# Descending columns in the projections' matmuls of a one-layer hybrid decoder trunk

## The chip, the cores and the metric

The kernel runs on one core of one Trainium2 chip. A core has five engines with instruction streams of their own: PE (TensorE, the 128 x 128 matmul array), DVE (VectorE), ACT (ScalarE), POOL (GpSimd) and SP (SyncE, which only issues transfers here). They work on SBUF, an on-chip memory of 128 partitions; PE writes its results to PSUM, eight banks of 512 fp32 columns in each partition. Off-chip memory is reached by DMA. The metric is the device time of one execution in microseconds (us), lower is better.

A matmul instruction has two operands. The stationary one (`lhsT`, 128 columns) is put into the array by a weight load, which the profile lists apart as PEld. The moving one (`rhs`, up to 512 columns) is then streamed past it column by column, and for every column that goes in, one column of results comes out and is written to, or added onto, a column of a PSUM bank. Where the moving columns are read and where the results go is told by two access patterns, each a start and a list of [step, count].

## The reference

One layer (`DEPTH` = 1), a batch of one, 256 tokens, width 1024, all in fp32. Three token mixers share one input projection; their outputs are gated and merged, and a squared-ReLU MLP with a gated per-layer embedding follows.

```python
proj = x @ w_in[i]                                   # 1024 -> 3528 columns
aq, ak, av, iq, ik, iw, bq, bk, bv, cq, ck, cv = jnp.split(proj, SPLIT_POINTS, axis=-1)
o_a = dsa_mixer(...)        # indexer, top-64 keys, 6 heads over one shared key/value head
o_b = dilated_mixer(...)    # 3 dilations x 4 slots
o_c = moba_mixer(...)       # one block of 256: plain causal attention, 6 heads
gates = jax.nn.sigmoid(x @ w_gate[i]).reshape(bsz, s_len, N_BRANCH, D_MODEL)
merged = (gates[:, :, 0] * (o_a @ w_br_a[i]) + gates[:, :, 1] * (o_b @ w_br_b[i])
          + gates[:, :, 2] * (o_c @ w_br_c[i]))
x = layer_norm(ALPHA * x + merged @ w_out[i], ln1_g[i], ln1_b[i])
h = jnp.square(jax.nn.relu(x @ w_up[i])) @ w_down[i]     # 1024 -> 4096 -> 1024
ple = jax.nn.sigmoid(x @ w_ple_gate[i]) * (p[i] @ w_ple[i])
x = layer_norm(ALPHA * x + h + ple, ln2_g[i], ln2_b[i])
```

By far the most arithmetic is in the products with weights: `w_in`, `w_gate`, `w_br_*`, `w_out`, `w_ple_gate`, `w_ple`, `w_up` and `w_down`. These are what the change calls the projections.

## The kernel before

Every fp32 product is computed from operands cut in two. `hi` is the value rounded to the array's reduced fp32 format (`F32R`), `lo` is what is left over, and a product a·b is the sum of three matmuls: hi·hi, hi·lo and lo·hi. Activations are cut once, when they are made. Weights are cut as they come in: the class `Weights` loads a unit of 128 x 1024 into one of five `raw` buffers (SP's DMA queue), ACT copies it with rounding to `whi` (L75), and DVE, in the first 58 units together with POOL, subtracts to get `wlo` (L79). `W.get` keeps four units ahead of the matmuls.

Nearly all matmuls come out of one helper, `prod` (L139 to L145), which emits the three matmuls of one 128 x 128 block: L141 hi·hi, L144 hi·lo and L145 lo·hi. Who calls it, in order of the program:

- `gemm`, for features and gates: stationary the weights, moving `xh`/`xl` (the transposed input, 256 tokens wide), results in one of three `mm` banks; `fill("c")` does the same with the mixers' outputs `op`.
- `values`, for the value heads: stationary the tokens, moving 328 or 384 weight columns.
- `merge` (256 columns), then the class `Wide` for `w_out` and the gate `w_ple_gate`, and the product with `w_ple`: stationary a tile of 128 tokens, moving 512 weight columns, results in banks that stay open over all eight blocks.
- The down projection (`onto`, `plain` and the last loop): stationary the hidden activations `hT`, moving 512 weight columns (a few 256). For 14 of the 32 hidden blocks, taken in pairs, it uses seven products in place of eight (Strassen-Winograd), with the sums made on DVE and POOL.

The up projection has its own two lines. At L825 `x1[:, :, k]` moves, 512 columns that are hi and lo of 256 tokens, so that one matmul does hi·hi and hi·lo into the two halves of a bank; at L827 the 256 hi columns move past the weights' `lo`. There the moving columns lie in two runs of 128 with a gap between them, and the results too.

Not through `prod` go the first four features (L429), the logits (L288), the transposes (L328, L676) and the product of probabilities and values (L332, L333).

The framework's scheduler sets the order of each engine's instructions when the kernel is built, and puts a semaphore wait ahead of an instruction wherever an operand was last touched elsewhere.

Of the kernel before, what the change touches and what calls it, by code (L numbers as in the profile page):

```python
# [98 lines left out]
def hybrid_layer(ctx: ExitStack, tc: tile.TileContext, x0, xn, pT, wqk, wva, wvb, wg, wbc, wba,  # L99
                 wout, wup, wdn, wpg, wple, lnrow, rel, onehot, pick, out):  # L100
    nc = tc.nc
    pe, act, dve, pool = nc.tensor, nc.scalar, nc.vector, nc.gpsimd
# [33 lines left out]

    pin = tc.keep_in_program_order

    def prod(ps, a, b, first, last, hold=False, more=False):  # L139

        i = pe.matmul(ps, lhsT=a[0], rhs=b[0], start=first, stop=False, skip_group_check=more)  # L141
        if hold:
            pin(i)
        pe.matmul(ps, lhsT=a[0], rhs=b[1], start=False, stop=False, skip_group_check=more)  # L144
        pe.matmul(ps, lhsT=a[1], rhs=b[0], start=False, stop=last, skip_group_check=more)  # L145

    def gemm(ps, units, xs, k=0):

        for u in units:
            hi, lo = W.get(u)  # L150
            for o in range(0, hi.shape[1], 128):
                prod(ps, (hi[:, o:o + 128], lo[:, o:o + 128]), xs[k], k == 0, k == len(xs) - 1)
                k += 1
# [57 lines left out]
    def mmbank(shape):  # L211
        t = mm.tile([128, 512], F32, name="mm", tag="mm")
        return t[:, 0:256] if shape == 256 else t
# [21 lines left out]
    def k_pair(a, b=None):  # L235


        k = (kp if b is None else k1).tile([128, 2, S], F32R, name="k", tag="k")
        for d, ps in ((slice(0, 128), a),) if b is None else ((slice(0, 64), a),
                                                             (slice(64, 128), b)):  # L240
            freed(act.copy(k[d, 0], ps),
                  dve.tensor_tensor(k[d, 1], ps, k[d, 0].bitcast(F32), op=ALU.subtract))
        return k
# [3 lines left out]
    def fill(what):  # L247


        for w in what:  # L250
            if w == "g":
                ps = mmbank(256)
                gemm(ps, u_g[n_g[0]], xs)
                freed(act.activation(G[:, n_g[0]], ps, AF.Tanh, scale=0.5))
                n_g[0] += 1
                continue
            f = n_c[0]
            n_c[0] += 1
            hi, lo = W.get(u_bc[f][0])
            ps = mmbank(512).rearrange("p (i s) -> p i s", i=2)  # L260
            for i, (k0, k1) in enumerate(((3, 5), (5, 8))):
                for k in range(k0, k1):
                    c = slice((k - 3) * 128, (k - 2) * 128)
                    prod(ps[:, i], (hi[:, c], lo[:, c]), (op[:, k, 0], op[:, k, 1]), k == k0,
                         k == k1 - 1)
            g = G[:, 3 * f + 1:3 * f + 3]
            freed(dve.scalar_tensor_tensor(g, g, 1.0, ps, op0=ALU.add, op1=ALU.mult))
            dve.tensor_tensor(g[:, 0], g[:, 0], g[:, 1], op=ALU.add)

    def feat(f):  # L270
        ps = mmbank(256)
        gemm(ps, u_q[f], xs)
        if f > 4:
            next(side, None)
        return ps
# [22 lines left out]
    def values(units, n, h0, heads, withiw):  # L298
        pss = [mmbank(512) for _ in range(2)]
        for i in range(4):  # L300
            hi, lo = W.get(units[i])
            for j in range(2):
                k = 2 * i + j
                c = slice(j * n, (j + 1) * n)
                for b in range(2):
                    t = slice(b * 128, (b + 1) * 128)
                    prod(pss[b][:, :n], (xh[:, k, t], xl[:, k, t]), (hi[:, c], lo[:, c]),
                         k == 0, k == KT - 1)
        v_out(pss, n, h0, heads, withiw)
# [98 lines left out]
    with ExitStack() as begin:  # L408
# [17 lines left out]
        for k in range(KT):  # L426
            for i, (w, x) in enumerate(((sh, xh), (sh, xl), (sl, xh))):
                for f in range(FIRST):
                    pe.matmul(first[f], lhsT=w[:, k, 128 * f:128 * f + 128], rhs=x[:, k],  # L429
                              start=k == i == 0, stop=k == KT - 1 and i == 2)  # L430
# [3 lines left out]
    ps = feat(4)  # L434
# [37 lines left out]
    for j in range(2):  # L472
        ps = feat(5 + 4 * j)
        k = k_pair(ps)
# [18 lines left out]
    for j in range(3):  # L493
        ps = feat(13 + 2 * j)
        k = k_pair(ps)
# [123 lines left out]
    x1 = p3.tile([128, 2, KT, 2, 128], F32R, name="x1", tag="x1")  # L619
# [68 lines left out]
    for i in range(4):  # L688
# [3 lines left out]
        b, cs = i // 2, H[i % 2]  # L692
        t = slice(b * 128, (b + 1) * 128)
        ps = mmbank(512)
# [79 lines left out]
    def load(i):  # L774

        wr[i] = r = xr[:, i % 2] if i else p3.tile([128, 2, D], F32, name="rows", tag="rows")
        k1, k2 = PAIRS[i]
        nc.sync.dma_start(r[:, 0], wdn[k1])
        for h in range(2):
            nc.sync.dma_start(r[:, 1, H[h]], wdn[k2, :, H[1 - h]])  # L780

    def form(i):

        t = p3.tile([128, 2, D], F32, name="rows", tag="rows") if i % 2 else Y
        wt[i] = t = t.rearrange("p b d -> p (b d)")
        r = wr[i].rearrange("p b d -> p (b d)")
        dve.tensor_tensor(t[:, 0:1024], r[:, 512:1536], r[:, 0:1024], op=ALU.subtract)
        dve.tensor_tensor(r[:, 512:1024], r[:, 1024:1536], t[:, 0:512], op=ALU.subtract)
        dve.tensor_tensor(t[:, 1024:1536], r[:, 1536:2048], r[:, 512:1024], op=ALU.subtract)
# [18 lines left out]
    def relu2(dst, ps):  # L808
        dve.tensor_reduce(dst, ps.rearrange("p b a t -> p b t a"), axis=AX.X, op=ALU.add)  # L809
        act.activation(dst, dst, AF.Relu)  # L810
        act.activation(dst, dst, AF.Square)  # L811
# [3 lines left out]
    for f in range(32):  # L815
        if f == 16:
            with tc.issue_after(W.loads[-1]):
                load(0)
            with tc.issue_after(W.subs[-1]):
                form(0)  # L820
        ps = mmbank(512).rearrange("p (b a t) -> p b a t", b=2, a=2)
        hi, lo = W.get(u_up[f][0])
        cs = [slice(k * 128, (k + 1) * 128) for k in range(KT)]
        for k, c in enumerate(cs):
            pe.matmul(ps, lhsT=hi[:, c], rhs=x1[:, :, k], start=k == 0, stop=False)  # L825
        for k, c in enumerate(cs):
            pe.matmul(ps[:, :, 0], lhsT=lo[:, c], rhs=x1[:, :, k, 0], start=False,  # L827
                      stop=k == KT - 1)
        if f not in half_of:
            spare = f % 2 == 0  # L830
            q = (p3.tile([128, 2, 128], F32, name="q1", tag="q1") if spare else
                 w2.tile([128, 8, 128], F32, name="a8", tag="a8")[:, 0:2])
            relu2(q, ps)
            q = q.rearrange("p b t -> p (b t)")
            act.copy(hT[f][:, 0], q)
            dve.tensor_tensor(hT[f][:, 1], q, hT[f][:, 0].bitcast(F32), op=ALU.subtract)
            continue
        j = half_of[f].index(f)
        if j == 0:
            a8 = w2.tile([128, 8, 128], F32, name="a8", tag="a8")  # L840
        relu2(a8[:, 2 * j:2 * j + 2], ps)
        if j == 0:
            continue

        a21, a11, a22, a12, *sums = (a8[:, j] for j in range(8))
        pool.tensor_tensor(sums[0], a21, a22, op=ALU.add)
        pool.tensor_tensor(sums[1], sums[0], a11, op=ALU.subtract)
        pool.tensor_tensor(sums[2], a11, a21, op=ALU.subtract)  # L848
        pool.tensor_tensor(sums[3], a12, sums[1], op=ALU.subtract)
        h = hT[half_of[f]]  # L850
        q = a8[:, 1:8].rearrange("p j t -> p (j t)")
        act.copy(h[:, 0], q)
        dve.tensor_tensor(h[:, 1], q, h[:, 0].bitcast(F32), op=ALU.subtract)
# [16 lines left out]
    def weights(u):  # L870
        w = W.get(u)
        while later:
            i = later.pop(0)
            load(i)
            form(i)
        return w
# [9 lines left out]
    for k in SEQ[:-2]:  # L886
# [3 lines left out]
        for u, terms in zip(u_dn[k], TERMS):  # L890
            hi, lo = weights(u)
# [27 lines left out]
    for i, acc in enumerate(ends):  # L919
        c = slice(256 * i, 256 * i + 256)  # L920
# [28 lines left out]
    for b in range(2):  # L949
        t = slice(128 * b, 128 * b + 128)  # L950
        for c, cs in enumerate(CUT[b]):
            for k in LATE:
                hi, lo = ws[k]
# [106 lines left out]
```

## Time and profile before

| | |
|---|---|
| median of 3 runs | 437.38 us (437.35 to 437.64) |
| the profiled execution | 437.87 us, of which 436.1 us span from first to last instruction |
| mean granted PE clock | 0.994 |
| PE / PEld busy | 426.1 / 385.7 us |
| DVE / ACT / POOL busy | 348.7 / 278.3 / 118.7 us |
| read from off-chip memory | 81.88 MB, 192 GB/s over the span |

A matmul's record begins when its columns begin to stream and ends, by a model, when the last result is in PSUM, so that records of neighbours overlap: a 256-column matmul is listed with about 283 ns, yet the next one begins 118 ns later. What a matmul costs in a row of matmuls is therefore the distance between starts, which the chain of waits shows, and not the mean length of a record. A weight load is listed with 188 ns and runs beside the matmul ahead of it.

### The profile page before, as it was taken

To read this page: it belongs to the slowest core of one execution; us is meant where nothing else is said; L and a number is where in the kernel's file an instruction comes from. 1 tells how busy PE (TensorE), PEld (TensorE's weight loads), DVE (VectorE), ACT (ScalarE), POOL (GpSimd) and SP (SyncE) were. 2 spreads that over 40 slices of the span, in tenths; PEclk is the share of its full clock that TensorE was granted. 3 is DMA by queue.
4 is the path that set the end of the run, shared out by engine and by line. 5 is a ranking of instruction groups with operands and counts; after the bars stand their busy time and mean duration, and the time that the engine had idled before them with its cause. 6 is when DMAs were issued, how large, how long until landed. Compare 5 with 4: busy or idle time off the path is not lost.

```text
span 436.1 us, 7738 instructions
## 1 busy us (share of the span) xinstructions
PE 426.1 (98%) x2804; PEld 385.7 (88%) x2804; DVE 348.7 (80%) x605; ACT 278.3 (64%) x499; POOL 118.7 (27%) x127
## 2 busy tenths in 40 slices
PE   8999999999999999999999999999999999999993
PEld 8989999999999999999887888888888888788883
DVE  5859967686576679979957879889988789899756
ACT  6767366486687786767605557877888746567310
POOL 1658246364533559400000002122420000000001
PEclk9999999999999999999999999999999999999997
DMA  8895966476544417478870686685665187556502
GB/s 286 303 318 147 259 218 205 144 222 226 171 142 151 128 47 220 122 222 331 260 273 5 197 290 207 198 287 172 197 190 192 39 299 238 162 180 203 183 2 96
DMA packets 28154, 84.28 MB, mean 193 GB/s; under 512 B 2976, under 2 KB 6984, under 8 KB 27732
## 3 DMA queue, kind: packets, MB, share of 16 engines
q1 hardware_dynamic: 26880, 79.54, 56.6%
q10 hardware_dynamic: 1140, 4.19, 3.1%
q8 instruction: 22, 0.36, 0.3%
q14 instruction: 16, 0.13, 0.1%
q0 software_dynamic: 96, 0.06, 0.0%
HBM read 81.88 MB, written 1.90 MB: 192 GB/s over the span
## 4 chain that ended last, share of the span: by engine, by line
PE 88%; DVE 7%; issue 2%; ACT 1%; POOLq 0%; POOL 0%; DVEq 0%; ACTq 0%
PE mm L825 14%; PE mm L141 12%; PE mm L144 11%; PE mm L145 11%; PE b L144 8%; PE b L141 8%; PE b L145 8%; PE mm L827 7%; PE b L429 3%; PE b L288 2%; DVE wlo L79 2%; PE b L328 1%; PE b L332 1%; PE b L135 1%; DVE idx L462 1%
## 5 line engine op out<-in xcount | busy, mean ns | idle before, releaser
L79 DVE TENSOR_TENSOR wlo<-raw,whi 128x1024 fp32r<-128x1024 f32 (+5 forms) x124 | 133.6, 1086 | 25.0 <-ACT whi L75 23.7
L75 ACT CAST whi<-raw 128x1024 fp32r<-128x1024 f32 (+3 forms) x124 | 123.4, 1004 | 47.1 <-PE b L145 19.6
L79 POOL TENSOR_TENSOR wlo<-raw,whi 128x384 fp32r<-128x384 f32 (+3 forms) x58 | 76.4, 1324 | 80.6 <-ACT whi L75 72.0
L141 PE MATMUL mm<-xh,whi 128*128 128x256 f32 x336 | 95.7, 285 | 0.0
L145 PE MATMUL mm<-xh,wlo 128*128 128x256 f32 x336 | 95.1, 283 | 0.0
L144 PE MATMUL mm<-xl,whi 128*128 128x256 f32 x336 | 95.1, 283 | 0.0
L825 PE MATMUL mm<-x,whi 128*128 128x512 f32 x256 | 64.2, 393 | 0.0
L141 PEld LDWEIGHTS mm<-xh,whi 128*128 128x128 f32 x336 | 63.3, 188 | 0.8
L144 PEld LDWEIGHTS mm<-xl,whi 128*128 128x128 f32 x336 | 63.3, 188 | 0.5
L145 PEld LDWEIGHTS mm<-xh,wlo 128*128 128x128 f32 x336 | 63.3, 188 | 0.3
L825 PEld LDWEIGHTS mm<-x,whi 128*128 128x128 f32 x256 | 45.8, 188 | 8.3
L642 POOL TENSOR_TENSOR rs<-rs,half 128x1 f32<-128x1 f32 x4 | 3.4, 843 | 151.6 <-DVE rs L641 151.6
L827 PEld LDWEIGHTS mm<-x,wlo 128*128 128x128 f32 x256 | 34.9, 188 | 2.7
L827 PE MATMUL mm<-x,wlo 128*128 128x256 f32 x256 | 35.5, 281 | 0.0
L144 PE MATMUL b<-wlo,store 128*128 128x512 f32 x84 | 32.8, 391 | 0.0
L145 PE MATMUL b<-whi,store 128*128 128x512 f32 x84 | 30.7, 389 | 0.0
L141 PE MATMUL b<-whi,store 128*128 128x512 f32 x84 | 27.7, 389 | 0.0
L848 POOL TENSOR_TENSOR a<-a 128x128 f32<-128x128 f32 x7 | 4.0, 565 | 58.2 <-ACT a L811 58.2
L809 DVE TENSOR_REDUCE a<-mm 128x256 f32<-128x512 f32 x23 | 15.8, 687 | 4.9 <-PE mm L827 4.6
L144 PEld LDWEIGHTS b<-wlo,store 128*128 128x128 f32 x84 | 15.8, 188 | 3.6 <-DVE wlo L79 0.4
L145 PEld LDWEIGHTS b<-whi,store 128*128 128x128 f32 x84 | 15.8, 188 | 3.2
L141 PEld LDWEIGHTS b<-whi,store 128*128 128x128 f32 x84 | 15.8, 188 | 3.2
(251 smaller groups left out, 874.5 us busy)
## 6 DMA issues: line engine op xcount, KB each, us to landing
raw<-in_wup_dram SPq DMA_DIRECT2D x32, 512.0 KB
raw<-in_wg_dram SPq DMA_DIRECT2D x24, 512.0 KB
raw<-in_wqk_dram SPq DMA_DIRECT2D x18, 512.0 KB
raw<-in_wdn_dram SPq DMA_DIRECT2D x18, 512.0 KB
raw<-in_wout_dram SPq DMA_DIRECT2D x8, 512.0 KB
raw<-in_wpg_dram SPq DMA_DIRECT2D x8, 512.0 KB
T<-tabd SPq DMA_DIRECT2D x24, 128.0 KB
xr<-in_wdn_dram SPq DMA_DIRECT2D x6, 512.0 KB
```

The source lines that it names most:

```text
L75: self.copies.append(nc.scalar.copy(hi, r).ins)
L79: i = e.tensor_tensor(lo[:, c], r[:, c], hi[:, c].bitcast(F32), op=ALU.subtract)
L135: pe.transpose(t[:, 0:128], ident, ident)
L141: i = pe.matmul(ps, lhsT=a[0], rhs=b[0], start=first, stop=False, skip_group_check=more)
L144: pe.matmul(ps, lhsT=a[0], rhs=b[1], start=False, stop=False, skip_group_check=more)
L145: pe.matmul(ps, lhsT=a[1], rhs=b[0], start=False, stop=last, skip_group_check=more)
L288: m = pe.matmul(ss[2 * n + h][:, QC[b]], lhsT=q[d, x, c], rhs=k[d, y, 0:128 * (b + 1)], start=i == 0, stop=i == 2)
L328: pe.transpose(t[:, 128 * i:128 * i + 128], P[:, 128 * i:128 * i + 128], ident)
L429: pe.matmul(first[f], lhsT=w[:, k, 128 * f:128 * f + 128], rhs=x[:, k], start=k == i == 0, stop=k == KT - 1 and i == 2)
L809: dve.tensor_reduce(dst, ps.rearrange("p b a t -> p b t a"), axis=AX.X, op=ALU.add)
L825: pe.matmul(ps, lhsT=hi[:, c], rhs=x1[:, :, k], start=k == 0, stop=False)
L827: pe.matmul(ps[:, :, 0], lhsT=lo[:, c], rhs=x1[:, :, k, 0], start=False, stop=k == KT - 1)
```

## The change

A new helper `back` turns every free dimension of an access pattern around, from its last element to its first. `prod` uses it on the result and on both moving operands, and the two lines of the up projection on theirs. Column j of the moving operand still gives column j of the result, so that the same numbers land in the same places; only the order in which a matmul goes through its columns is the opposite one. Stationary operands, the weight loads, the matmuls that don't go through `prod`, and all reads and writes by other engines stay as they are.

```diff
     pin = tc.keep_in_program_order
 
+    def back(x):
+
+        return x[(slice(None), *[slice(None, None, -1)] * (len(x.shape) - 1))]
+
     def prod(ps, a, b, first, last, hold=False, more=False):
 
+        ps, b = back(ps), [back(x) for x in b]
         i = pe.matmul(ps, lhsT=a[0], rhs=b[0], start=first, stop=False, skip_group_check=more)
         if hold:
             pin(i)
@@ -822,9 +827,9 @@
         for k, c in enumerate(cs):
-            pe.matmul(ps, lhsT=hi[:, c], rhs=x1[:, :, k], start=k == 0, stop=False)
+            pe.matmul(back(ps), lhsT=hi[:, c], rhs=back(x1[:, :, k]), start=k == 0, stop=False)
         for k, c in enumerate(cs):
-            pe.matmul(ps[:, :, 0], lhsT=lo[:, c], rhs=x1[:, :, k, 0], start=False,
+            pe.matmul(back(ps[:, :, 0]), lhsT=lo[:, c], rhs=back(x1[:, :, k, 0]), start=False,
                       stop=k == KT - 1)
```

In the built program the change reaches 2405 of the 2803 matmuls: 631 at each of the three lines of `prod` (412 with 256 moving columns, 16 with 328, 16 with 384 and 187 with 512), 256 at the up projection's first line (512 columns) and 256 at its second (256 columns). Their patterns now begin at the last column and have the step -1, and the two-run patterns of the up projection step from run to run by -2048 and -256 elements. On every engine the instructions stand in the same order as before. Of the semaphore waits some differ: PE has 34 waits on matmuls of its own where it had 24, all on a matmul at least 27 places earlier in its own stream, DVE has 103 waits on PE where it had 113, and PE and DVE have two instructions more each that do nothing but wait. The change adds five lines ahead of the body, so that L141, L144, L145, L825 and L827 are L146, L149, L150, L830 and L832 afterwards.

As an example of the waits, PE's stream where a feature's accumulation begins in a fresh `mm` bank, before:

```order
L145 MATMUL mm<-xh,wlo 128x256
L141 MATMUL mm<-xh,whi 128x256 [waits DVE_49]
L144 MATMUL mm<-xl,whi 128x256
L145 MATMUL mm<-xh,wlo 128x256
L141 MATMUL mm<-xh,whi 128x256
```

and the same place after the change:

```order
L150 MATMUL mm<-xh,wlo 128x256
L146 MATMUL mm<-xh,whi 128x256 [waits DVE_49,PE_49]
L149 MATMUL mm<-xl,whi 128x256
L150 MATMUL mm<-xh,wlo 128x256
L146 MATMUL mm<-xh,whi 128x256
```

`DVE_49` and `PE_49` are the counters of finished instructions of the two engines. The matmuls stand as before; the first one of the bank now also waits for the matmul of PE's own that last wrote that bank.

## The prediction

> **What bounds the kernel now.** I read the page's busy shares and its chain of waits first, then the busy time by stage.
>
> ```profile
> span 436.1 us, 7738 instructions
> PE 426.1 (98%) x2804; PEld 385.7 (88%) x2804; DVE 348.7 (80%) x605; ACT 278.3 (64%) x499; POOL 118.7 (27%) x127
> PE 88%; DVE 7%; issue 2%; ACT 1%; POOLq 0%; POOL 0%; DVEq 0%; ACTq 0%
> PE mm L825 14%; PE mm L141 12%; PE mm L144 11%; PE mm L145 11%; PE b L144 8%; PE b L141 8%; PE b L145 8%; PE mm L827 7%; PE b L429 3%; PE b L288 2%; DVE wlo L79 2%; PE b L328 1%; PE b L332 1%; PE b L135 1%; DVE idx L462 1%
> ```
>
> The first row alone would not do, since a matmul's record ends by a model and records overlap. The third says it better: 88% of the chain that ended last is PE, and by the fourth 79% of the span lies on the very five lines that the change edits. PE waits for hardly anyone; this is the whole list of its waits:
>
> ```profile
> PE b L135 <- POOL ident masks.py:199: 1.7, 1, 1.7
> PE b L332 <- DVE pt L330: 0.6, 1, 0.6
> PE b L288 <- DVE q L231: 0.5, 1, 0.5
> ```
>
> By stage (start:end, length, then busy time of PE, PEld, DVE, ACT and POOL, granted clock):
>
> ```profile
> 17.60:145.00 127.40, 126.94 (x1071) 122.73 (x1070) 93.34 (x245) 85.56 (x184) 69.01 (x61) 1.00 0.65 200
> 145.00:180.00 35.00, 34.38 (x291) 32.68 (x291) 28.80 (x68) 25.37 (x62) 19.42 (x19) 1.00 0.48 145
> 256.70:346.00 89.30, 89.30 (x514) 78.36 (x513) 78.40 (x98) 70.07 (x121) 17.17 (x28) 1.00 0.61 187
> 346.00:436.10 90.10, 82.88 (x382) 68.82 (x380) 74.10 (x88) 42.20 (x49) 1.80 (x2) 0.97 0.50 170
> ```
>
> PE is full in every stage at a full clock, and DVE, the next, has 6 us (145 to 180) to 34 us (17.6 to 145) to spare. The last row lacks 7 us of PE, the final layer norm and store behind the last matmul. So a matmul that gets dearer is paid for in full, with no cover; one that stays as it is leaves the time where it is.
>
> **The change part by part.** No instruction is added on any engine's data path and none is moved. Three things differ: the rate of 2405 matmuls, what they cost to begin, and some waits.
>
> *The rate.* The step from one start to the next is in the chain of waits (start, length, what), here for 256 columns in one run (L144, L145), 512 columns (L825), 256 columns in two runs (L827), and the transposes of 128 columns (L676):
>
> ```profile
> 60.95 0.12 PE mm L145
> 61.53 0.12 PE mm L144
> 243.15 0.87 PE mm L676 x8
> 256.76 1.82 PE mm L825 x8
> 258.59 0.94 PE mm L827 x8
> 259.53 1.86 PE mm L825 x8
> 261.39 0.95 PE mm L827 x8
> ```
>
> 512 columns take 1.84 / 8 = 0.230 us, 256 take 0.945 / 8 = 0.118 us, so 256 more columns cost 0.112 us: 0.4375 ns a column, and 0.118 - 0.112 = 6 ns a matmul beside its columns. The changed matmuls stream 3 x (412 x 256 + 16 x 328 + 16 x 384 + 187 x 512) = 637,824 columns in `prod` and 256 x 512 + 256 x 256 = 196,608 in the up projection, 834,432 in all: 365 us, and 2405 x 6 ns = 14 us with it. That 379 of 436 us hangs on them agrees with the chain. The counts are those of the trace:
>
> ```profile
> 0.00:436.10 436.10, 189.86 (x631) 118.71 (x631) 0.99 0.60 193
> 0.00:436.10 436.10, 64.18 (x256) 45.79 (x256) 0.99 0.60 193
> 0.00:436.10 436.10, 35.47 (x256) 34.91 (x256) 0.99 0.60 193
> ```
>
> (whole span, busy PE and PEld, for L141, L825 and L827.)
>
> No matmul of this trace walks downward, so the price of a descending column is to be bounded. From below it is zero: PE gives a column every 0.4375 ns in the ascending order at a granted clock of 1.00, and the same columns pass through the same array, so that an order cannot make it stream faster. The nearest row is L827, whose columns lie in two runs, 2048 elements apart where they are read and 256 where they are written: it takes 0.118 us as the one-run matmuls of L144 and L145 do (0.12), so a break in the walk in the middle of a matmul costs nothing visible. A walk with a jump at every element is to be seen on DVE alone, in rows by form:
>
> ```profile
> L809 DVE TENSOR_REDUCE a<-mm 128x256 f32<-128x512 f32 x23 | 15.8, 687 | 4.9 <-PE mm L827 4.6
> L267 DVE SCALAR_TENSOR_TENSOR G<-G,mm 128x512 f32<-128x512 f32 x8 | 5.4, 673 | 0.0
> ```
>
> L809 reads 512 PSUM columns in 687 ns, going to and fro between two places 128 elements apart; L267 reads 512 in their order in 673 ns. Jumping costs DVE 2%. But DVE goes at 1.3 ns an element, a third of PE's pace, so this shows that the memory doesn't mind the order, and not that PE's path keeps its pace.
>
> From above: the slowest stream of columns that PE shows is the transpose's. Eight of 128 columns take 0.87 us, 109 ns each, 0.85 ns a column, nearly twice the matmul's. If a descending walk made PE handle columns singly at that pace, the price would be 0.85 - 0.4375 = 0.4125 ns a column, 834,432 x 0.4125 ns = 344 us.
>
> I take zero, the lower end, since L827 is the nearest row, PE's own, in the very stage that the change edits, and a step of -1 touches the same neighbours in turn as a step of +1. Both ends stay in the range.
>
> Two rules of the Trainium skill pull in opposite directions here. The Trainium skill's "SBUF — State Buffer", section "Door 1: The DMA port swizzle", says that memory lines of 16 bytes give full bandwidth as long as consecutive accesses fall into one line; four fp32 columns share a line in either direction, so by it the reading side adds 0 us. The Trainium skill's "PSUM — Partial Sum Buffer", section "Specifications (TRN2)", says that PSUM's lines hold 8 bytes and that any pattern that isn't contiguous slows matmuls significantly. Whether -1 counts as contiguous it does not say: if what matters is that pairs share a line, the sum stays at 0 us; if it is the step +1, it is the second rival below. No run here shows either so far; L827 with its two runs only says that one break does not count.
>
> *The beginning of a matmul.* The 6 ns beside the columns may change when a pattern begins at its end. From below it is again 0. From above I take a doubling, 2405 x 6 ns = 14 us; nothing in the trace asks for it, since L144, L825 and L827 begin at different offsets and in different shapes with the same few ns.
>
> *The waits.* PE gets ten more waits on matmuls of its own, each at least 27 places back. At 0.118 us a step 27 places are 3.2 us, against a matmul record of under 0.4 us, so each is long met when PE reaches it: 0 us. What is queued behind them is PE's own stream, and if I am wrong by one matmul's length each, 0.28 us, the ten cost 2.8 us. The records' lengths:
>
> ```profile
> L144 PE MATMUL mm<-xl,whi 128*128 128x256 f32 x336 | 95.1, 283 | 0.0
> L825 PE MATMUL mm<-x,whi 128*128 128x512 f32 x256 | 64.2, 393 | 0.0
> ```
>
> Two instructions on PE that only wait: at most one step each, 2 x 0.118 = 0.24 us, and I take 0.1 us. DVE's two more and ten fewer lie beside PE's work, with the 6 to 34 us to spare; without that cover, at DVE's 0.3 to 0.7 us per piece in the one stretch where the chain runs through it (below), they would be worth under 1 us either way.
>
> The sum: 0 + 0 + 0.1 us against the profiled execution's 437.87 us, which is 436.1 us of span and 1.8 us around it. The median of the runs shown is 437.38, 0.1% below that execution; the forecast is for a median, so 437.4 us.
>
> **The rivals.** *The half pace* (slower). Descending columns are not taken in pairs, on the read or the write side, and each of the 2405 matmuls streams at the transpose's 0.85 ns a column. The place is PE's stream in every stage, and since nothing covers it, it decides from the first nanosecond: 437.9 + 344 = 782 us. DVE and ACT, at 349 and 278 us busy, would then wait for PE throughout. For it: the ascending stream is so much faster than any other stream of fp32 in this trace (0.4375 ns against 1.3 on DVE and 0.85 in the transposes) that it may live on pairing neighbours, and a pair found by "the next address" is not found downward. Against it: L827, and DVE's indifference. The rule of the Trainium skill's "PSUM — Partial Sum Buffer", section "Specifications (TRN2)", is this rival's, if it counts -1 as not contiguous.
>
> *A dearer beginning* (slower). The pace holds and only the 6 ns double: 437.9 + 14 = 452 us. For it: nothing but that the change touches 2405 beginnings. Against it: three shapes with one price. Anything between 0.2% and a tenth I count here.
>
> *Fewer waits on the chain* (faster). From 145 to 180 us the chain leaves PE; these are four of its pieces there:
>
> ```profile
> 160.11 0.34 issue
> 163.24 0.51 issue
> 169.60 0.60 issue
> 175.55 0.35 issue
> ```
>
> If DVE's ten dropped waits emptied these, 1.8 us would go from the chain, but PE is 34.38 of 35.00 us busy there, so that at most 0.6 us comes through, 436.8 us: within what I call no change. To go further, PE's waits would have to fall as well, and they rise.
>
> *The change doesn't do what it says.* Operand and result are turned together, so a later step of the build could turn both back. Then the time is the old one, 437.4 us, for another reason; the trace cannot tell this apart from my forecast, only a matmul with one side turned could.
>
> **How the numbers follow.** A measurement of this kernel can tell about 0.2% from no change, 0.9 us. No change in the pace: 0.54, with 0.02 of it for the pattern that is turned back; half pace 0.29, about half as much, since no row shows a descending column at PE's pace and two only come near; a dearer beginning 0.13; faster by more than 0.2%: 0.04. So faster 0.04, same 0.54, slower 0.42. The forecast is 437.4 us, and its own range, from the waits' bounds, 436.6 to 438.3. That and the dearer beginning hold 0.7, which isn't enough, so the range has to reach the half pace: 436.6 to 785 us.
>
> **What would show it.** Right: L830 in eights of 1.82 to 1.86 us and L832 of 0.94 in the chain, the 256-column steps at 0.12 us, PE busy still 426 us, no row for PE waiting on PE. Half pace: L830 in eights of about 3.5 us, L832 about 1.8, PE records longer by 110 to 220 ns, the clock still 1.00, ACT and DVE at the same busy time with long waits on PE. A dearer beginning: the same few ns more for 256 columns as for 512. A wait on the path: a list of waits with PE in both places. The forecast is wrong if the two lengths' difference is no longer 0.112 us: then columns, not instructions, have changed their price.

## The result and the profile after

The changed kernel takes 441.27 us (median of 4 runs, 440.56 to 442.21), the kernel before 437.45 us (4 runs). The ratio is 1.0088, with a 95% interval of 1.0068 to 1.0109: slower by 0.88%, or 3.8 us. The profiled execution took 442.21 us with a span of 440.4 us, 4.3 us over that of before.

The page's busy time and its chain by engine and line, after:

```profile
span 440.4 us, 7742 instructions
PE 429.6 (98%) x2804; PEld 385.3 (87%) x2804; DVE 349.3 (79%) x605; ACT 278.5 (63%) x499; POOL 118.4 (27%) x127
PE 78%; DVE 10%; issue 3%; ACT 1%; POOLq 0%; DVEq 0%; POOL 0%
PE mm L830 14%; PE mm L146 10%; PE mm L150 10%; PE mm L149 10%; PE b L146 8%; PE b L150 8%; PE b L149 8%; PE mm L832 7%; DVE wlo L79 3%; PE b L293 2%; DVE idx L467 1%; PE b L333 1%; DVE m L466 1%; DVE idx L457 1%; PE b L337 1%
```

PE is busy 3.5 us longer, every other engine is within 0.6 us of its busy time before. The chain now runs through DVE more (10% for 7%), but that alone does not mean that DVE has become the bound: PE is busy 98% as before. The whole list of PE's waits, after:

```profile
PE b L135 <- POOL ident masks.py:199: 1.7, 1, 1.7
PE b L293 <- DVE q L236: 1.3, 1, 1.3
PE b L337 <- DVE pt L335: 0.6, 1, 0.6
```

No wait of PE on itself is in it, and the waits sum to 3.6 us where they were 2.8: 0.8 of the 4.3 us between the two profiled executions. The other 3.5 us have to be in the matmuls. Their steps (from the start of one matmul to the start of the next) are in the chain of waits (start, length, what). Before, four 512-column matmuls of the output projection into an open bank:

```profile
207.21 0.91 PE b L145 x4
```

and after, the same place and the up projection:

```profile
207.62 0.93 PE b L150 x4
258.43 1.86 PE mm L830 x8
260.29 0.94 PE mm L832 x8
261.24 1.87 PE mm L830 x8
263.11 0.94 PE mm L832 x8
```

The rounded 0.91 and 0.93 are worth a second look in a longer stretch. Before, a row of the output projection's four began at 207.21 us and the next such row follows 2.72 us later, twelve matmuls of 227 ns; after, 2.79 and 2.81 us later, twelve of 233:

```profile
209.93 0.91 PE b L145 x4
212.65 0.91 PE b L145 x4
```

```profile
210.43 0.93 PE b L150 x4
213.22 0.93 PE b L150 x4
```

Taken over all neighbours of equal shape in the two traces, the mean distance between starts (distances over 0.4 us left out) is:

| moving columns | where | before, ns | after, ns | matmuls | change, us |
|---|---|---|---|---|---|
| 512, one run | `prod` | 229.0 (L145 to L144 alone: 227.1) | 234.7 (233.3) | 561 | +3.2 |
| 512, read in two runs | up projection, first line | 230.0 | 233.7 | 256 | +0.9 |
| 384 | `values` | 176.7 | 180.0 | 48 | +0.2 |
| 256, one run | `prod` (mean of three lines) | 121.0 | 120.5 | 1236 | -0.6 |
| 256, in two runs | up projection, second line | 118.9 | 117.7 | 256 | -0.3 |

That sums to +3.4 us (the 48 matmuls with 328 columns add under 0.1), against the 3.5 us by which PE is busy longer; the medians of all runs lie 3.8 us apart. The means hold a few longer gaps; the medians of `prod` are 227 and 233 ns at 512 columns, 117 and 118 at 256. So a wide descending matmul costs 3 to 6 ns more, a 256-column one in the mean slightly less, and there are enough wide ones to lose by it.

### The profile page after: what moved, and what is told of

It reads as the page before. It is cut to its first block, busy times and chain, and to the rows that moved or that the text cites. A ratio compares the mean times of both kernels' runs of the same rounds, so it can differ in the third digit from the quotient of the medians.

```text
span 440.4 us, 7742 instructions
## 1 busy us (share of the span) xinstructions
PE 429.6 (98%) x2804; PEld 385.3 (87%) x2804; DVE 349.3 (79%) x605; ACT 278.5 (63%) x499; POOL 118.4 (27%) x127
## 4 chain that ended last, share of the span: by engine, by line
PE 78%; DVE 10%; issue 3%; ACT 1%; POOLq 0%; DVEq 0%; POOL 0%
PE mm L830 14%; PE mm L146 10%; PE mm L150 10%; PE mm L149 10%; PE b L146 8%; PE b L150 8%; PE b L149 8%; PE mm L832 7%; DVE wlo L79 3%; PE b L293 2%; DVE idx L467 1%; PE b L333 1%; DVE m L466 1%; DVE idx L457 1%; PE b L337 1%
## 5 line engine op out<-in xcount | busy, mean ns | idle before, releaser
L146 PE MATMUL mm<-xh,whi 128*128 128x256 f32 x336 | 95.9, 285 | 0.0
L150 PE MATMUL mm<-xh,wlo 128*128 128x256 f32 x336 | 95.3, 284 | 0.0
L149 PE MATMUL mm<-xl,whi 128*128 128x256 f32 x336 | 95.2, 283 | 0.0
L830 PE MATMUL mm<-x,whi 128*128 128x512 f32 x256 | 65.1, 397 | 0.0
L146 PEld LDWEIGHTS mm<-xh,whi 128*128 128x128 f32 x336 | 63.2, 188 | 0.9 <-PE mm L150 0.2
L149 PEld LDWEIGHTS mm<-xl,whi 128*128 128x128 f32 x336 | 63.2, 188 | 0.5
L150 PEld LDWEIGHTS mm<-xh,wlo 128*128 128x128 f32 x336 | 63.2, 188 | 0.3
L830 PEld LDWEIGHTS mm<-x,whi 128*128 128x128 f32 x256 | 46.0, 188 | 8.9
L832 PEld LDWEIGHTS mm<-x,wlo 128*128 128x128 f32 x256 | 34.6, 188 | 2.9
L832 PE MATMUL mm<-x,wlo 128*128 128x256 f32 x256 | 35.4, 282 | 0.0
L149 PE MATMUL b<-wlo,store 128*128 128x512 f32 x84 | 33.4, 397 | 0.0
L150 PE MATMUL b<-whi,store 128*128 128x512 f32 x84 | 31.4, 397 | 0.0
L146 PE MATMUL b<-whi,store 128*128 128x512 f32 x84 | 28.3, 397 | 0.0
L150 PEld LDWEIGHTS b<-whi,store 128*128 128x128 f32 x84 | 15.8, 188 | 3.8
L146 PEld LDWEIGHTS b<-whi,store 128*128 128x128 f32 x84 | 15.8, 188 | 3.7
L149 PEld LDWEIGHTS b<-wlo,store 128*128 128x128 f32 x84 | 15.8, 188 | 3.7
```

The costliest lines, as they stand in the source:

```text
L830: pe.matmul(back(ps), lhsT=hi[:, c], rhs=back(x1[:, :, k]), start=k == 0, stop=False)
L832: pe.matmul(back(ps[:, :, 0]), lhsT=lo[:, c], rhs=back(x1[:, :, k, 0]), start=False, stop=k == KT - 1)
```

## The experiments

Three theories stood at the start. *Wide*: a descending matmul costs about 6 ns more with 512 columns and nothing with 256. *Waits*: the loss is in the added semaphore waits. *Spread*: a few ns on each of the 2405, the rival of the dearer beginning. Medians of the kernel before in these comparisons are 437.59 to 437.61 us. The edits of the first four runs are shown against the changed kernel, that of the last against the kernel before, with parts left out.

**Wide ones alone.**

```diff
-        ps, b = back(ps), [back(x) for x in b]
+        if ps.shape[-1] > 256:
+            ps, b = back(ps), [back(x) for x in b]
@@ up projection, second line
-            pe.matmul(back(ps[:, :, 0]), lhsT=lo[:, c], rhs=back(x1[:, :, k, 0]), start=False,
+            pe.matmul(ps[:, :, 0], lhsT=lo[:, c], rhs=x1[:, :, k, 0], start=False,
```

> Only matmuls with more than 256 moving columns go downward (593 in the helper, with 328, 384 or 512 columns, and the 256 of the up projection's first line); the 1492 with 256 columns go upward again. Theory 'wide' (a descending matmul costs about 6 ns more where it has 512 columns, nothing at 256): the whole loss stays, 441.3 us. Rival 'waits' (the loss is in PE's ten added waits on its own matmuls, most of which stand at the first matmul of a fresh bank with 256 columns): 437.5 us. Rival 'spread' (a few ns on each of the 2405): 437.45 + 3.8 x 849 / 2405 = 438.8 us.

(The counts in that text are wrong: 657 matmuls in `prod` and 256 in the up projection make 913, so that *spread* stands at 438.9 us.) Measured: 441.78 us, ratio 1.0105 (1.0088 to 1.0122). The whole loss and a little more: *wide* holds, *waits* and *spread* do not.

**Narrow ones alone.**

```diff
-        ps, b = back(ps), [back(x) for x in b]
+        if ps.shape[-1] <= 256:
+            ps, b = back(ps), [back(x) for x in b]
@@ up projection, first line
-            pe.matmul(back(ps), lhsT=hi[:, c], rhs=back(x1[:, :, k]), start=k == 0, stop=False)
+            pe.matmul(ps, lhsT=hi[:, c], rhs=x1[:, :, k], start=k == 0, stop=False)
```

> The other half: only the 1492 matmuls with 256 columns go downward. 'Wide': 437.5 us, no change. 'Waits': about 441 us. 'Spread': 437.45 + 3.8 x 1492 / 2405 = 439.8 us... (1236 in the helper and 256 at the up projection's second line: 1492; 'wide' needs their step to stay at 0.118 us.)

Measured: 436.15 us, ratio 0.9969 (0.9959 to 0.9978). None of the three had this: it is faster than the kernel before. A second comparison of the same kernel:

> The same kernel as in e2: both sides descending for the 1492 matmuls with 256 columns alone. If the gain seen there (0.9969 of the kernel before) is real: 436.2 us against 437.6, an interval wholly under 0.998.

436.47 us, ratio 0.9975 (0.9964 to 0.9985). The interval is not wholly under 0.998, as its expectation had it, but it is clear of 1: a gain of 1.1 to 1.5 us. Its chain in the up projection (the 512-column line L831 ascending, L833 descending):

```profile
256.23 1.82 PE mm L831 x8
258.05 0.94 PE mm L833 x8
258.99 1.83 PE mm L831 x8
260.82 0.94 PE mm L833 x8
```

Before, the eights of L825 took 1.82 and 1.86 us in turn; here every one takes 1.82 or 1.83. In the mean the first line's step falls from 230.0 to 228.4 ns though its own columns still ascend, and the second line's from 118.9 to 117.4: 0.4 us each over 256 matmuls. With 0.2 us at the 384-column matmuls (176.7 to 173.4 ns) and about 0.5 us at the 1236 others of 256 columns (121.0 to 120.6), that makes some 1.5 us. A good part of it thus lies at matmuls that were not turned; the 384-column step stands at 173.5 ns in the last experiment too, where nothing is turned, so that at least this part can't be put down to the direction.

**Which side.** Only the read turned, for all 2405:

```diff
-        ps, b = back(ps), [back(x) for x in b]
+        b = [back(x) for x in b]
@@ up projection, both lines: result as before the change, rhs turned
```

> Only the moving operand is read downward, results are written upward, for all 2405 matmuls; the columns of each product come out in the opposite order, so the output is not the reference's. If the cost is on the reading side: 441.3 us, with 512-column steps of 233 ns. If it is on the writing side: 437.5 us and 227 ns. If it needs both: 437.5 us here and in the next run. If each side has a part: between.

Measured: 441.11 us, ratio 1.0084 (1.0067 to 1.0101). Only the write turned (`ps = back(ps)`, `b` left alone, and the like in the up projection):

> Only the results are written downward, the moving operand is read upward; the columns of each product come out in the opposite order, so the output is not the reference's. If the cost is on the writing side: 441.3 us, with 512-column steps of 233 ns; if on the reading side: 437.5 us and 227 ns.

Measured: 437.58 us, ratio 1.0008 (0.9997 to 1.0018). Chain of waits with the read turned:

```profile
206.20 0.93 PE b L150 x4
257.00 1.87 PE mm L830 x8
258.86 0.94 PE mm L832 x8
```

and with the write turned:

```profile
207.05 0.91 PE b L150 x4
256.61 1.82 PE mm L830 x8
258.44 0.94 PE mm L832 x8
259.38 1.86 PE mm L830 x8
261.24 0.95 PE mm L832 x8
```

With the write turned the steps are those of before, down to the 1.82 and 1.86 in turn; with the read turned they are those of the changed kernel. Writing PSUM downward costs nothing here. These two runs settle the waits as well: the added waits come with the results' patterns, so that the second run has all of them (34 of PE on itself, two instructions on PE that only wait) and the first has none, with the counts of the kernel before.

The gain of the narrow ones was taken apart in the same way. Read only:

> Of these 1492 matmuls only the read goes downward, results are written upward, so that columns come out in the opposite order and the output is not the reference's. All semaphore waits are those of the kernel before. If the gain of e2 comes from the read (256 columns in 118.3 ns in place of 120): about 436.2 us here too. If it comes from the waits that turned results change: 437.5 us.

436.13 us, ratio 0.9971 (0.9962 to 0.9979). Write only:

> Of these 1492 matmuls only the write goes downward (output not the reference's, as in e7). The semaphore waits are those of e2: DVE has 101 on PE where it had 113 before, PE 30 on itself where it had 24, and PE and DVE have one and two fewer instructions that only wait. If the gain of e2 comes from the waits: 436.2 us; if from the read: 437.5 us.

437.66 us, ratio 1.0004 (0.9994 to 1.0014). The gain comes with the turned read; the waits have no part in it.

**The steps by themselves.** The layer is left out; matmuls run alone, 36 to a row, each row into one bank, all from the same operands. What is called fp32 here is `F32R`, as in the kernel. This kernel and the one under the next heading were executed once each.

```python
for w in (128, 32):                                   # stationary columns
    for n in (512, 448, 384, 320, 256, 192, 128):     # moving columns
        for name, turn_r, turn_p in (("up", 0, 0), ("down", 1, 1), ("rd", 1, 0), ("wr", 0, 1),
                                     ("alt", 2, 2)):
            ...  # 36 matmuls: pe.matmul(p, lhsT=wt[:, 0:w], rhs=r), r and p turned or not
```

> Matmuls alone, in rows of 36 into one bank, all with the same operands, nothing else running; the layer is left out. Rows named up (both sides ascending), down (both descending), rd (only the read descending), wr (only the write descending) and alt (every other matmul descending), for 512, 448, 384, 320, 256, 192 and 128 columns, first with a stationary operand of 128 columns, then of 32. Theory 'fee' (each descending matmul begins about 6 ns later, and at 256 columns this hides under the next weight load): with 128 stationary columns, down is 6 ns over up at 512, 448 and 384 columns and 0 at 256 and less; with 32 stationary columns, whose load is short, down is 6 ns over up at 256 and 192 columns as well. Theory 'width' (the price grows with the columns beyond about 300): down minus up is 0 at 256 with either stationary width, about 1 ns at 320, 3.5 at 384, 6 at 512. Theory 'company' (the descending matmul only loses against other engines' traffic): down equals up everywhere here. If alternating matmuls are shorter than up, a kernel that alternates would beat both. Further rows: reads with a step of 2 and 4 elements, and with bf16 operands 512 and 256 columns up, down, rd, wr, and a write with a step of 2 elements.

The timeline of PE (start, length, line, result and operands, stationary, moving shape, count); the step is the distance to the next row's start over 36:

```profile
17.86 8.32 PE L48 MATMUL up<-mv,wt 128*128 128x512 f32 x36
26.02 8.57 PE L48 MATMUL down<-mv,wt 128*128 128x512 f32 x36
34.42 8.56 PE L48 MATMUL rd<-mv,wt 128*128 128x512 f32 x36
42.82 8.35 PE L48 MATMUL wr<-mv,wt 128*128 128x512 f32 x36
51.00 8.67 PE L48 MATMUL alt<-mv,wt 128*128 128x512 f32 x36
154.68 4.48 PE L48 MATMUL up<-mv,wt 128*128 128x256 f32 x36
158.99 4.43 PE L48 MATMUL down<-mv,wt 128*128 128x256 f32 x36
163.26 4.42 PE L48 MATMUL rd<-mv,wt 128*128 128x256 f32 x36
385.67 4.26 PE L48 MATMUL up<-mv,wt 128*32 128x256 f32 x36
389.76 4.40 PE L48 MATMUL down<-mv,wt 128*32 128x256 f32 x36
394.00 4.40 PE L48 MATMUL rd<-mv,wt 128*32 128x256 f32 x36
```

At 512 columns up takes 8.16 / 36 = 0.2267 us, down and rd 0.2333, wr 0.2272. At 256 columns up takes 4.31 / 36 = 0.1197, down 0.1186: here descending is the cheaper one, as in the kernel. With 32 stationary columns it is the other way, 0.1136 up and 0.1178 down. The steady steps, from the starts of the last 24 of a row, in ns:

| moving columns | up, 128 stationary | down | up, 32 stationary | down |
|---|---|---|---|---|
| 512 | 226.7 | 233.3 | 231.7 | 233.3 |
| 448 | 202.7 | 206.7 | 202.2 | 204.5 |
| 384 | 173.3 | 177.8 | 173.3 | 175.5 |
| 320 | 146.7 | 146.7 | 143.3 | 146.7 |
| 256 | 120.0 | 118.3 | 113.3 | 117.8 |
| 192 | 111.7 | 111.7 | 88.3 | 88.9 |
| 128 | 111.7 | 111.6 | 60.0 | 60.0 |

*Company* falls: the 6.7 ns are there with nothing else running. *Fee* falls: with a short weight load nothing is hidden, and the difference is 1.7 ns at 512 and 0.6 at 192, not a constant 6. *Width* falls too, since at 256 the difference is 4.5 ns with 32 stationary columns and -1.7 with 128. What the last column does show is a straight line: with 32 stationary columns, descending, 64 more columns cost 28.9 ns all the way, 0.4514 ns a column. Ascending steps with 32 stationary columns lie 0 to 4.5 ns under that line, in no order that the width explains. With 128 stationary columns nothing goes below 111.6 ns, which looks like the weight load's own pace, since with 32 stationary columns the floor is not there (60.0 ns at 128); 256 columns stand just above it. Alternating directions gains nothing (236.7 at 512 columns).

The rows with other steps and with bf16 bear on the half pace:

```profile
240.95 8.57 PE L48 MATMUL rbroad<-mv,wt 128*128 128x256 f32 x36
249.34 8.52 PE L48 MATMUL up<-mv,wt 128*32 128x512 f32 x36
466.49 7.96 PE L48 MATMUL bup<-mb,wb 128*128 128x512 bf16 x36
474.29 7.93 PE L48 MATMUL bdown<-mb,wb 128*128 128x512 bf16 x36
497.60 4.09 PE L48 MATMUL bup<-mb,wb 128*128 128x256 bf16 x36
501.53 4.09 PE L48 MATMUL bdown<-mb,wb 128*128 128x256 bf16 x36
513.33 7.93 PE L48 MATMUL bpskip<-mb,wb 128*128 128x256 bf16 x36
```

`rbroad` reads 256 fp32 columns with a step of 4 elements: 8.39 / 36 = 0.233 us, twice the 0.120 of neighbouring columns; with a step of 2 it is 0.230. `bpskip`, with bf16 operands, writes 256 columns with a step of 2: 0.216 us, twice the 0.109 of `bup`. So the half pace exists on both sides, the read measured in fp32 and the write in bf16. It belongs to steps that leave elements out; a step of -1 has none of it. In bf16 the direction costs nothing: 0.2158 us at 512 columns and 0.1092 at 256, up and down.

**Where a read begins.** The same kind of kernel with the first column moved within the tile (one of its loops; the widths in between, 96 and 64 stationary columns and two moving operands in turn are left out):

```python
for o in (1, 2, 3, 4, 6, 8, 16, 32, 64, 256):         # rows upa .. upj, downa .. downj
    both(512, o, 128, "up" + c, "down" + c)           # rhs = mv[:, o:o + n]
    both(256, o, 128, "up" + c, "down" + c)
```

> Matmuls alone as in e5, rows of 30, layer left out. First 512 down to 256 columns in steps of 16, up and down. Then 512 and 256 columns with the first column 1, 2, 3, 4, 6, 8, 16, 32, 64 and 256 elements into the tile (rows named upa to upj and downa to downj). Then 96 and 64 stationary columns, and two moving operands in turn. Theory 'line' (a descending read is dearer because of where it begins within a memory line): ascending rows that begin 1, 2 or 3 elements in take 233 ns at 512 columns too, and some descending ones 227. Theory 'rate' (a descending fp32 read streams at 0.451 ns a column always, and an ascending one gains on it here and there): descending rows lie on one line over the widths, 7.2 ns a step of 16 columns, and are the same at every start; ascending rows lie on or under that line.

Timeline rows, 30 to a row (f: 8 elements in, i: 64):

```profile
302.40 7.16 PE L43 MATMUL upf<-mv,wt 128*128 128x512 f32 x30
309.39 7.17 PE L43 MATMUL downf<-mv,wt 128*128 128x512 f32 x30
316.39 3.67 PE L43 MATMUL upf<-mv,wt 128*128 128x256 f32 x30
319.90 3.70 PE L43 MATMUL downf<-mv,wt 128*128 128x256 f32 x30
365.81 7.01 PE L43 MATMUL upi<-mv,wt 128*128 128x512 f32 x30
372.65 7.17 PE L43 MATMUL downi<-mv,wt 128*128 128x512 f32 x30
379.66 3.77 PE L43 MATMUL upi<-mv,wt 128*128 128x256 f32 x30
383.26 3.72 PE L43 MATMUL downi<-mv,wt 128*128 128x256 f32 x30
```

Eight elements in, 512 columns take 6.99 / 30 = 0.2330 us up and 0.2333 down: the advantage of ascending is gone, and 256 columns take 0.1170 up. Sixty-four in, it is back: 0.2280 up, 0.2337 down. Over all eleven starts, the steady step at 512 columns is 226.7 to 227.5 ns up at 0, 64 and 256 elements and 228.9 to 236.6 up at the eight others; down it is 233.3 to 235.6 but for two starts (3 and 32 elements) at 240. Both theories hold in part only. A start off a 16-byte line (1 or 2 elements) does make the ascending read as dear as the descending one, but so does one that lies on a line (8 elements), and one 3 elements in does not (228.9). And descending steps are nearly, not wholly, the same at every start; over the widths, with 128 stationary columns, they lie within 2.5 ns of the line above. With two moving operands in turn 512 columns take 226.7 ns up and 233.3 down, as with one; with 96 and 64 stationary columns 230 and 233.3. What the ascending read has at 512 columns is a gain that it gets in full at the three starts tried that are multiples of 64 elements, and the descending read at none of the eleven. Why, these runs don't show.

**A better start in the kernel.** The last experiment tried to use that: ascending columns, with the tiles that move 256 columns at a time beginning 8 elements further in.

```diff
-    xh = p1.tile([128, KT, S], F32R, name="xh")
-    xl = p1.tile([128, KT, S], F32R, name="xl")
+    xh, xl = (p1.tile([128, KT * S + 64], F32R, name=n)[:, 8:8 + KT * S]
+              .rearrange("p (k s) -> p k s", k=KT) for n in ("xh", "xl"))
@@ and op in the same way
```

> The kernel before, all columns ascending, but the tiles xh, xl and op, which move past the weights 256 columns at a time, begin 8 elements (32 bytes) further into memory. In e9 a 256-column ascending matmul whose columns begin 8 elements in took 116.7 ns in place of 120, less than a descending one (118.3). If the start decides in the kernel as it does alone: up to 1200 x 3.3 ns = 4.0 us less, 433.6 us. If the kernel's steps, which change their stationary operand with every matmul and stand at 117 to 118 ns already, have that gain by chance: about 437.5 us. If they hold to the 116.7 ns: 1200 x 1 ns less, 436.4 us.

Measured: 438.19 us, ratio 1.0017 (1.0007 to 1.0026), a little slower than all three cases. The mean steps at 256 columns, by the line of the second of two neighbours, rose from 120.5, 122.4 and 120.1 ns (L141, L144, L145) to 121.6, 123.7 and 121.1, their medians from 117 and 118 to 120. The start matters in the kernel, but not as it does alone, where the stationary operand never changed. What sets these few ns, perhaps how the read of the moving columns falls in with the weight load's, is not settled by these runs.

## Why the prediction was right or wrong

The time lies in the stated range (436.6 to 785 us), but that range spans every rival up to the half pace, and none of them is what happened: that the time fell inside is luck. The forecast's own range, 436.6 to 438.3 us, missed 441.27. The case taken as likeliest, no change, did not come; the kernel is slower by four times the 0.2% that a measurement can tell. The 0.42 for slower was the part that came true, for a reason that neither of its two rivals gave.

*What bounds the kernel*: right. The loss is paid in full by PE: 3.4 us of steps in the traces, 3.8 us of time. Nothing covered it. (DVE's room was less than the 6 us stated: from 180 to 207 us, a stage that the prediction does not list, it was busy for 23.97 of 27.00. Nothing hung on it.)

*The rate*: this step failed. The price of a descending column was put at zero because L827 was "the nearest row" and a break in its walk cost nothing visible. But L827 has 256 columns, and at that width, with 128 stationary columns, the direction does not cost anything either: in the steps by themselves (`e5_steps`) 118.3 ns descending for 120.0 ascending, where 512 columns take 233.3 for 226.7. A row that could have warned stood beside it. L825, 512 columns read in two runs, took 1.82 and 1.86 us for eight in turn, in one shape and one direction. The cheaper eight comes to 228 ns a matmul, near the 227 of the one-run matmuls of 512 columns, so that the break is not what costs; in the dearer one single steps reach 236. The prediction took the mean, 0.230 us, for the price of that width and did not ask why it moved. By its own last criterion it is wrong in this point: the difference between 512 and 256 columns was to stay 0.112 us and is (1.87 - 0.94) / 8 = 0.116.

Neither end of the rate was a bound. The lower one, that an order cannot make the columns stream faster, is contradicted by the 256-column reads just named. The upper one, 0.85 ns a column, was read from the transposes' 109 ns for 128 columns. In `e5_steps` a plain ascending matmul of 128 columns takes 111.6 ns with 128 stationary columns and 60.0 with 32, so that the transposes' row need not mean a slower stream, and the 344 us rested on it alone. What did come near that pace is a step that skips elements, 230 ns for 256 columns.

*The beginning of a matmul*: the rival "a dearer beginning" had the measured size in its band (0.2% to a tenth) and the wrong mechanism. It asked for the same few ns at 256 as at 512 columns; the runs show +6 and -0.5 in `prod`, and the 1492 narrow matmuls alone make the kernel faster. The 6 ns themselves were not a price of beginning: on the straight line of `e5_steps`, 60.0 - 128 x 0.4514 leaves 2.2 ns beside the columns.

*The half pace*: did not come. Of the reasons against it, that a step of -1 touches the same neighbours in turn fits the runs; DVE's indifference to jumps does not carry over, since PE halves its pace when it skips. What is doubled is a step that skips elements, read (0.230 for 0.120 us) or written (0.216 for 0.109). The rule weighed for this rival (the prediction calls it the second there, it is the first) is that of the Trainium skill's "PSUM — Partial Sum Buffer", section "Specifications (TRN2)", that a non-contiguous pattern slows matmuls significantly. The trace agrees for a write with a step of 2, and a step of -1 is not slowed: writing downward measured 1.0008 (0.9997 to 1.0018).

The other rule, of the Trainium skill's "SBUF — State Buffer", section "Door 1: The DMA port swizzle", gave 0 us for the reading side, and it is the reading side that costs. Measurement decides against it twice: descending fp32 columns take 233.3 ns at 512 columns against 226.7, and a read with a step of 2, which meets each 16-byte line twice, takes 230 ns at 256 columns against 120 for neighbouring ones.

*The waits*: right, 0 us. With all of them added and the reads left alone the kernel measured 437.58 us against 437.61.

*The pattern turned back by a later step*: excluded. Turning the read alone moves the steps, so it reaches the chip. With the write alone turned, the columns come out in the opposite order of the read; had a later step made of that an ascending write and a descending read, the steps would be the 233 ns of the turned read, and they are 227.

## What to carry to other kernels

A matmul's moving columns may be read and written from last to first where an algorithm wants it: in these runs the price was nothing in bf16, nothing on the PSUM side, and at most 5% of a step for fp32 reads; a step that skips elements halved the pace. Where PE is full, look for a few ns at each width apart, and in a row of the same width as the matmuls at stake: with 128 stationary columns, 128 and 192 moving ones took the same 111.6 ns, and such a row cannot show what its columns cost. Turning only the 256-column matmuls around gave 0.9975 (0.9964 to 0.9985) of the kernel before and beats both kernels here, but it rests on a gain of about 1 ns a step whose cause is open, and part of it fell on matmuls that were not turned.

## What the runs showed of the hardware that was not expected

- The read of fp32 moving columns is what the direction touches, and not the accumulating write: 441.11 us with the read turned, 437.58 with the write turned.
- With 32 stationary columns a descending fp32 read lies on one straight line from 128 to 512 columns, 0.4514 ns a column, 8% above the 0.416 ns a column that bf16 shows (215.8 - 109.2 ns over 256 columns). Ascending fp32 reads lie 0 to 4.5 ns below it.
- At 512 columns the ascending read's gain depends on where it begins: 226.7 to 227.5 ns at 0, 64 and 256 elements, 228.9 to 236.6 at eight other starts.
- Reading every second or every fourth fp32 element costs the same doubling, 230 and 233 ns for 256 columns.
